# Half of a merge ahead of its last norms, a router that counts before it places, and a table product in the router's chain

## The chip, the cores and the metric

One Trainium2 chip, one core. The metric is the device time of one execution in microseconds, the median of several runs. The profiler takes one execution for the traces. TensorE (PE) does the matrix products, VectorE (DVE) and ScalarE (ACT) the elementwise work, GpSimd (POOL) index patterns and masks, SyncE (SP) issues most of the DMA transfers.

## The reference

256 tokens of width 1024 go through one block with a two-way recurrence, a neighbourhood attention and a mixture of 16 experts, and then through two further blocks. What bears on the change is this, in short:

```python
# first block
ya = rwkv_out(y, ...)               # per-head group norm of y (8 heads of 64), bonus, gate
x  = x + m2 * ((sigmoid(z9) * (ya @ proj_a) + sigmoid(z10) * (yb @ proj_b)) @ w_out)   # the merge
h2 = modulate(rms_norm(x), m3, m4)
x  = x + m5 * moe(h2, router_w, router_bias, w1, w3, w2)
# moe: scores = sigmoid(h2 @ router_w); the best of 4 expert groups, then its 2 best experts of 4;
# gate weights are the chosen scores, divided by their sum
for i in range(2):                  # the two further blocks
    h = h + mixer(rmsnorm(h))       # pooling and dilated attention
    h = h + square(relu(rmsnorm(h) @ w_up[i])) @ w_down[i]
    gate = sigmoid(rmsnorm(h) @ w_gate[i])
    h = h + gate * (p[i] @ w_ple[i])   # p: 256 tokens x 256, a table that depends on no earlier result
```

Everything is float32 on both sides.

## The kernel before

The stages follow each other on one core: the inputs' norm and the attention, the recurrence with the gate products and the second branch's projection beside it, the merge, the router and the experts, and then mixer, feed-forward and gate of the two further blocks.

**Precision.** A product of float32 accuracy is made as three fast products (`mm3`, L119 to L121) of operands that were split into a high part (ACT) and a rest (DVE). `split` (L127, L128) does this for small pieces; `prepare` (L180, L181) for the large weights, 128 x 2048 at a time, that `plan` lists and `advance` loads through SP's queue (L166). Some small products are plain float32 instead; the profile shows two records for each of those.

**Order.** A planner orders each engine's instructions by the order of emission and its own estimate of their times, so that text order is not engine order. `tc.issue_after(i)` forces a group of instructions behind `i` on the engine of `i`. Tiles with the same tag share a fixed number of buffers; a load into a tag waits until the oldest user is done.

**Recurrence and norms.** `rwkv` runs generators in turn: three slots of the recurrence, `gates` (gate products, L985 to L1024, a PSUM bank "gg"), `factors`, and `rwkv_out`. The latter makes four norms (`norm(t, g)`, L896 to L922: t is the token half, g the head group): PE transposes y, DVE and ACT normalise, PE transposes back (L918), and ACT and DVE split the result into `yaT` (L940, L941). The order is (1,0), (0,0), (1,1), (0,1), each as soon as its two units of the recurrence are past.

**Merge.** `merge` (L1139) multiplies `yaT` by `proj_a` in 4 column quarters q and 2 depth halves k2, `product(q, k2)` (L1146), 12 fast products each, 96 in all. The k2 = 0 products need only the norms with g = 0. Quarter by quarter, DVE and ACT then form `mT` (L1173 to L1176), `halves` multiplies it by `w_out`, and `done` adds the result to x. `feed` and `route` (L1737, L1749) transpose the new x and multiply it by the router's weights; `lg` are the router's logits.

**Router and experts.** `router` (L1205) is a chain of small DVE steps that ends with the mask of the chosen experts (`chose`) and the gate weights. `moe` (L1245) makes from it, with five plain products on PE, each token's place in its expert's list and the count by which an expert has more than 64 tokens (`more`). All engines then pass a branch on that count (L1293), behind which the overflow code lies. `experts` (L1406) prepares the gather: the rest of x's split (`rest`, L1428) and one-hot matrices from the places (`choose`, L1435), both ahead of the branch in the text, and then gathers the tokens of an expert group by products with the one-hots (L1461). `second_masks` makes masks for the mixer of the further blocks on POOL, in the text ahead of the gather. The transposes of x that start the experts' sums (L1268) stand ahead of the router in the text.

**Gate of a further block.** `second_gate` (L2001) loads p[i], transposes it (four transposes, L214), multiplies it by `w_ple_2[i]` in two column halves (24 products of 512 columns for both token halves), and uses these in `done` when the gate's own products end.

## Time and profile before

| what | value |
|---|---|
| median of 3 runs | 1576.36 us (1572.23, 1576.36, 1580.75) |
| the profiled execution | 1566.17 us |
| its span | 1564.5 us |
| mean granted TensorE clock | 0.966 of full speed |
| PE busy | 1457.9 us (93%), 10562 instructions |
| DVE busy | 889.1 us (57%), 1869 instructions |
| ACT busy | 634.8 us (41%), 1035 instructions |
| POOL busy | 306.6 us (20%), 316 instructions |
| moved by DMA | 274.21 MB |

The span is the time from the first to the last instruction of the profiled execution. In the rows of the trace, a line such as `L181 DVE TENSOR_TENSOR wl<-wr,wh 128x2048 fp32r<-128x2048 f32` names the line of the kernel, the engine, the operation, and output and inputs with partitions, elements and type. A bracket behind a row of the timeline tells how long the engine stood idle before and what released it. PEclk and the digits of the slices are shares of full speed and of the slice. DMA share is the mean busy share of the 16 DMA engines.

### The profile page before, as it was taken

How to read it: one execution, taken by the hardware profiler on the slowest of the kernel's cores; microseconds unless marked ns; L12 is line 12 of the kernel's file. 1: busy time of each engine (PE TensorE's matmuls, PEld its weight loads, DVE VectorE, ACT ScalarE, POOL GpSimd, SP SyncE). 2: the span in 40 equal slices, each digit the busy share in tenths (PEclk: the TensorE clock that was granted, in tenths of full speed). 3: DMA queues.
4: the chain of work that ended last, by engine and by line, in shares of the span. 5: the costliest groups of instructions: out<-in, count | busy, mean ns of one | idle time of the engine just before them, and what ended most of it. 6: DMA issues, size and time to landing. Idle time of an engine off the chain costs nothing.

```text
span 1564.5 us, 26010 instructions
## 1 busy us (share of the span) xinstructions
PE 1457.9 (93%) x10562; PEld 1113.8 (71%) x10562; DVE 889.1 (57%) x1869; ACT 634.8 (41%) x1035; POOL 306.6 (20%) x316
## 2 busy tenths in 40 slices
PE   6899999999999886689999899999999999999996
PEld 3677777778788675543443368699988887998885
DVE  3778458676766676622311255565556755755555
ACT  2433545444454452110110145554444645544443
POOL 1002049765666410490000000000000000000000
PEclk9899999898999897889999999999999999999999
DMA  9511223222232133689999935355554452555542
GB/s 325 162 42 66 68 84 122 79 80 73 69 94 77 56 134 129 258 331 420 421 419 421 380 98 173 108 170 185 186 187 168 155 197 87 183 189 188 188 162 74
DMA packets 118328, 274.21 MB, mean 175 GB/s; under 512 B 8591, under 2 KB 31795, under 8 KB 106935
## 3 DMA queue, kind: packets, MB, share of 16 engines
q1 hardware_dynamic: 115608, 270.13, 49.1%
q10 hardware_dynamic: 2559, 2.32, 0.5%
q8 instruction: 85, 1.39, 0.4%
q14 instruction: 44, 0.36, 0.1%
q0 software_dynamic: 32, 0.00, 0.0%
HBM read 271.36 MB, written 1.06 MB: 174 GB/s over the span
## 4 chain that ended last, share of the span: by engine, by line
PE 54%; DVE 1%; ACT 1%; issue 0%; DVEq 0%; ACTq 0%
PE mm L119 12%; PE mm L120 12%; PE mm L121 12%; PE mm L1476 11%; PE mm L1461 1%; PE mm L1619 1%; PE mm L1540 1%; PE mm L1876 1%; PE mm L1737 1%; PE mm L1895 1%; PE mm L1849 0%; PE mm L1905 0%; PE mm L214 0%; PE mm L1838 0%; DVE wl L181 0%
## 5 line engine op out<-in xcount | busy, mean ns | idle before, releaser
L181 DVE TENSOR_TENSOR wl<-wr,wh 128x2048 fp32r<-128x2048 f32 (+2 forms) x130 | 271.6, 2089 | 208.1 <-ACT wh L180 195.7
L180 ACT ACTIVATE wh<-wr 128x2048 fp32r<-128x2048 f32 (+2 forms) x130 | 227.2, 1749 | 160.7 <-PE mm L121 108.1
L121 PE MATMUL mm<-xTh,wl 128*128 128x256 f32 x512 | 143.9, 281 | 0.0
L120 PE MATMUL mm<-xTl,wh 128*128 128x256 f32 x512 | 143.7, 281 | 0.0
L119 PE MATMUL mm<-xTh,wh 128*128 128x256 f32 x512 | 143.2, 281 | 0.0
L119 PE MATMUL mm<-wh,fh 128*128 128x512 f32 x256 | 101.4, 396 | 0.0
L121 PE MATMUL mm<-wh,fl 128*128 128x512 f32 x256 | 101.1, 395 | 0.0
L120 PE MATMUL mm<-wl,fh 128*128 128x512 f32 x256 | 101.0, 395 | 0.0
L300 POOL TENSOR_SCALAR mr<-mr,silu_c 128x512 f32<-128x512 f32 x56 | 97.8, 1747 | 5.3 <-DMA mr<-in_mod_w_dram 5.1
L120 PEld LDWEIGHTS mm<-xTl,wh 128*128 128x128 f32 x512 | 96.2, 188 | 0.9 <-DVE xTl L941 0.3
L119 PEld LDWEIGHTS mm<-xTh,wh 128*128 128x128 f32 x512 | 96.1, 188 | 0.7
L119 PE MATMUL mm<-wh,xTh 128*128 128x512 f32 (+1 forms) x272 | 95.7, 352 | 0.7 <-ACT big L1813 0.5
L121 PEld LDWEIGHTS mm<-xTh,wl 128*128 128x128 f32 x512 | 96.3, 188 | 0.0
L120 PE MATMUL mm<-wl,xTh 128*128 128x512 f32 (+1 forms) x272 | 93.0, 342 | 0.0
L121 PE MATMUL mm<-wh,xTl 128*128 128x512 f32 (+1 forms) x272 | 92.5, 341 | 0.0
L301 POOL TENSOR_TENSOR mra<-mra,mr 128x512 f32<-128x512 f32 x56 | 74.0, 1322 | 4.2
L823 ACT ACTIVATE nt<-mm 128x512 f16<-128x512 f32 x80 | 47.6, 595 | 59.3 <-PE mm L837 51.8
L119 PEld LDWEIGHTS mm<-wh,xTh 128*128 128x128 f32 x272 | 51.2, 188 | 8.6 <-ACT big L1813 0.7
L121 PEld LDWEIGHTS mm<-wh,fl 128*128 128x128 f32 x256 | 48.1, 188 | 11.5
L120 PEld LDWEIGHTS mm<-wl,fh 128*128 128x128 f32 x256 | 48.1, 188 | 10.7
L119 PEld LDWEIGHTS mm<-wh,fh 128*128 128x128 f32 x256 | 48.1, 188 | 10.6
L121 PEld LDWEIGHTS mm<-wh,xTl 128*128 128x128 f32 x272 | 51.2, 188 | 6.2
(569 smaller groups left out, 3496.4 us busy)
## 6 DMA issues: line engine op xcount, KB each, us to landing
wr<-in_w_up_dram SPq DMA_DIRECT2D x32, 1024.0 KB, 5.6
wr<-in_w_down_dram SPq DMA_DIRECT2D x32, 1024.0 KB, 5.1
wr<-in_w_in_dram SPq DMA_DIRECT2D x22, 1024.0 KB, 5.1
wr<-in_moe_w_dram SPq DMA_DIRECT2D x21, 1024.0 KB, 8.7
wh<-in_moe_w_dram SPq DMA_DIRECT2D x20, 1024.0 KB, 13.8
wl<-in_moe_w_dram SPq DMA_DIRECT2D x20, 1024.0 KB, 12.0
mr<-in_mod_w_dram SPq DMA_DIRECT2D x64, 256.0 KB, 2.8
wx<-in_moe_w_dram SPq DMA_DIRECT2D x14, 1024.0 KB, 10.3
```

Source lines behind the costliest of these rows:

```text
L119: mm(out, l.hi, r.hi, start=start, stop=False, **kw)
L120: mm(out, l.hi, r.lo, start=False, stop=False, **kw)
L121: mm(out, l.lo, r.hi, start=False, stop=stop, **kw)
L180: self.nc.scalar.activation(w.hi, raw, AF.Copy)
L181: self.nc.vector.tensor_tensor(w.lo, raw, w.hi.bitcast(F32), op=ALU.subtract)
L300: nc.gpsimd.tensor_scalar(raw, raw, self.sc[:, k, 0:1], None, op0=ALU.mult)
L301: nc.gpsimd.tensor_tensor(acc, acc, raw, op=ALU.add)
L823: nc.scalar.activation(nt, v4(bz), AF.Copy)
L1461: mm(b[:, k * 256:k * 256 + 256], part[:, t, 2 * q + k, :], sel[:, t].rearrange("p j c -> p (j c)"), start=(i == 0), stop=(i == 3))
L1476: mm(b[r], lT[:, k0 + k, c0 + SLOT * j:c0 + SLOT * j + SLOT], w[:, k], start=(start and k == 0), stop=(stop and k == n - 1))
L1540: mm(acc[2 * n + k // 2][:, k % 2], part[:, k * P:(k + 1) * P], back, start=False, stop=(g == 7 and part is y.lo), skip_group_check=True)
L1619: mm(banks[t], first[:, k, t * P:(t + 1) * P], w[:, k, :], start=(k == 0), stop=False)
```

## The change

1. `merge` is taken apart into `merge_piece` (load and split a piece of `proj_a`) and `merge_product`. The four k2 = 0 products are issued in `rwkv_out`: two behind the first two norms, and one each with the third and the fourth. The norms now begin only when `gates` is past. The pieces have three split buffers instead of two.
2. The splits of the `w_out` weights (`prepare`) stand behind the last norm's own split.
3. The first further block's table product p[0] @ w_ple[0] moves ahead: p[0] is loaded at the start of the recurrence, w_ple[0] in the merge into tiles that the norms use until then, and eight plain float32 products run on PE behind the last `route`. ACT copies them out and stores them to DRAM; `second_gate(0)` loads them back in one transfer, and its transposes, products and weights are gone.
4. In `moe` the overflow count comes ahead of the places; x's transposes stand behind the place products; the gate weights are made behind the branch, and inside it for the overflow.
5. In `experts`, four of the eight `rest` steps are free, two stand behind the choice and two behind the one-hots; the one-hots of the first group are behind the branch, and `second_masks` behind the first gather.

The diff, cut to its core:

```diff
@@ rwkv_out
-            self.split_into(self.yaT[:, 2 * g:2 * g + 2, t * P:(t + 1) * P],
-                            b[:, 0:256].rearrange("p (k t) -> p k t", k=2))
+            dst, b = self.yaT[:, 2 * g:2 * g + 2, t * P:(t + 1) * P], b[:, 0:256].rearrange("p (k t) -> p k t", k=2)
+            self.normed = [nc.scalar.activation(dst.hi, b, AF.Copy).ins,
+                           tt(dst.lo, b, dst.hi.bitcast(F32), op=ALU.subtract).ins]
...
-        while not {("prep", d, g, i), "bonus"} <= self.past:
+        while not {("prep", d, g, i), "bonus", "gates"} <= self.past:
             yield
...
+        yield from until((0, 0, 3), (1, 0, 2))
+        yield from norm(1, 0)
+        yield from until((0, 0, 2), (1, 0, 3))
+        yield from norm(0, 0)
+        self.pieces = [self.merge_piece(fp, n) for n in range(3)]
+        for q, tag in enumerate(("gg", "nn1")):
+            self.merge_product(fp, q, 0, tag)
+            yield
+        yield from until((0, 1, 3), (1, 1, 2))
+        self.merge_product(fp, 2, 0, "nn2")
+        yield from norm(1, 1)
+        yield from until((0, 1, 2), (1, 1, 3))
+        self.merge_product(fp, 3, 0, "nn0")
+        yield from norm(0, 1)
@@ gates (three places: w of the gate products, of proj_b, and the end)
-                wt = self.split(pool, raw, [P, 2, 256], "w", bufs=2)
+                wt = self.split(pool, raw, [P, 2, 256], "w", bufs=3)
...
+        self.past.add("gates")
@@ merge
+    def merge_product(self, fp, q, k2, tag=None):
+        if tag:
+            self.merged.append(self.bank(tag, 1))
+        wt, b = self.pieces.pop(0), self.merged[q]
+        for k in range(2):
+            for j in range(2):
+                self.mm3(b[:, 256 * j:256 * j + 256], wt[:, k, j * P:(j + 1) * P], self.yaT[:, 2 * k2 + k, :],
+                         start=(k2 == k == j == 0), stop=(k2 == 1 and k == 1), skip_group_check=True)
+        n = 4 * k2 + q + 3
+        if n < 8:
+            self.pieces.append(self.merge_piece(fp, n))
...
+        for n in range(2):
             for k in range(2):
+                nc.sync.dma_start(ple[n][k], a["w_ple_2"][0][k * P:(k + 1) * P, 512 * n:512 * n + 512])
...
+        with self.tc.issue_after(self.normed[0]), self.tc.issue_after(self.normed[1]):
+            self.prepare()
...
+        self.ple = self.dram.tile([T, D], F32, name="pled")
+        for n in range(2):
+            banks = [self.bank(("nn1", "nn2")[t], 1) for t in range(2)]
+            with self.tc.issue_after(self.routed):
+                for t in range(2):
+                    for k in range(2):
+                        nc.tensor.matmul(banks[t], pT[:, k, t * P:(t + 1) * P], ple[n][k], start=(k == 0), stop=(k == 1))
+            for t in range(2):
+                o = fb.tile([P, 512], F32, tag=("mr", "mra")[n and t], name="pleo", bufs=(3, 1)[n and t])
+                nc.scalar.activation(o, banks[t], AF.Copy)
+                nc.scalar.dma_start(self.ple[t * P:(t + 1) * P, 512 * n:512 * n + 512], o)
@@ moe
+        score, mask = self.router(pool)
         left, more = pool.tile([1, 16], I32, name="left"), pool.tile([1, 1], I32, name="more")
         b = self.bank("mn")
         mm(b[:, 0:16], ones, mask[:, 0], start=True, stop=False)
         mm(b[:, 0:16], ones, mask[:, 1], start=False, stop=True)
         ts(left, b[0:1, 0:16], -float(SLOT), 0.0, op0=ALU.add, op1=ALU.max)
-        nc.vector.tensor_reduce(more, left, axis=AX.X, op=ALU.max)
+        found = nc.vector.tensor_reduce(more, left, axis=AX.X, op=ALU.max).ins
+
+        b = self.bank("mn")
+        mm(b[:, 0:16], tri, mask[:, 0], start=True, stop=True)
+        mm(b[:, 16:32], ones, mask[:, 0], start=True, stop=False)
+        placed = mm(b[:, 16:32], tri, mask[:, 1], start=False, stop=True).ins
+        place = pool.tile([P, 2, 16], F32, name="place")
+        with self.tc.issue_after(found):
+            stt(place, b[:, 0:32].rearrange("p (t e) -> p t e", t=2), 1.0, mask, op0=ALU.add, op1=ALU.mult)
+            ts(place, place, -1.0, None, op0=ALU.add)
+        with self.tc.issue_after(placed):
+            for k in range(8):
+                for t in range(2):
+                    mm(acc[k // 2][:, k % 2, t * P:(t + 1) * P], self.x[:, t, k * P:(k + 1) * P], self.ident,
+                       start=(k % 2 == t == 0), stop=False, skip_group_check=True)
...
-        run(self.second_masks(self.lys[1].tile([P, 8, T], F32R, tag="xTl", name="cmask", bufs=1).bitcast(F32)))
+        self.gate = self.weighed(pool0, score, mask)
         run(main)
@@ experts
+        rest(0, range(4))
         with self.tc.issue_after(self.chose):
-            rest(0)
+            rest(1, range(2))
+        yield
         with self.tc.issue_after(choose(0)):
-            for q in range(1, 4):
-                rest(q)
-        yield
+            rest(1, range(2, 4))
         for q in range(4):
             gather(0, q)
+
+        mask = self.lys[1].tile([P, 8, T], F32R, tag="xTl", name="cmask", bufs=1).bitcast(F32)
+        begin = nc.gpsimd.tensor_copy(mask[:, 7, 0:1], state["g", 0, 1][:, 3, 0:1]).ins
+        with self.tc.issue_after(begin):
+            run(self.second_masks(mask))
@@ second_gate
+        if i:
+            pt = ...
+        else:
+            done_ahead = pool.tile([P, 2, D], F32, name="ple")
+            nc.scalar.dma_start(done_ahead, self.ple[:, :].rearrange("(t p) d -> p t d", p=P))
...
+                if i == 0:
+                    state[t] = done_ahead[:, t, 512 * n:512 * n + 512]
+                    continue
```

## Rows read from the trace of the kernel before

**Rows 1.** The page's slices, 39.1 us each: TensorE's busy share in tenths.

```profile
PE   6899999999999886689999899999999999999996
```

**Rows 2.** Windows by stage; columns: window, length, busy by engine, PEclk, DMA share, GB/s.

```profile
576.00:606.00 30.00, 11.65 (x72) 10.11 (x73) 21.55 (x60) 8.63 (x11) 0.00 (x0) 0.63 0.76 265
...
604.00:617.00 13.00, 12.70 (x91) 12.57 (x92) 6.78 (x12) 4.69 (x8) 0.00 (x0) 0.85 0.20 62
...
617.00:644.00 27.00, 26.69 (x133) 21.73 (x132) 15.35 (x30) 5.99 (x10) 0.00 (x0) 1.00 0.45 161
...
650.00:657.00 7.00, 1.81 (x17) 1.61 (x15) 6.04 (x28) 2.28 (x2) 6.31 (x11) 0.91 1.01 411
...
720.00:730.00 10.00, 10.00 (x54) 4.52 (x54) 2.31 (x4) 1.83 (x3) 0.00 (x0) 1.00 1.01 418
...
1210.00:1214.00 4.00, 4.00 (x19) 3.25 (x18) 2.37 (x10) 2.08 (x2) 0.00 (x0) 1.00 0.63 194
```

**Rows 3.** Timeline of VectorE, tail and merge: start, us, instruction, idle before.

```profile
576.05 0.68 DVE L1024 SCALAR_TENSOR_TENSOR gt<-gt,mm 128x512 f32<-128x512 f32 x1
...
587.92 0.42 DVE L790 TENSOR_TENSOR y<-y,mm 128x256 f32<-128x256 f32 x1 [0.91 <-PE mm L784]
...
588.33 2.28 DVE L181 TENSOR_TENSOR wl<-wr,wh 128x2048 fp32r<-128x2048 f32 x1
...
605.41 0.42 DVE L941 TENSOR_TENSOR yaTa<-mm,yaTw 128x256 fp32r<-128x256 f32 x1 [1.26 <-ACT yaTw L940]
...
616.63 0.68 DVE L1176 TENSOR_TENSOR mTv<-mu,mTk 128x512 fp32r<-128x512 f32 x1
```

**Rows 4.** Timeline of TensorE, from the tail to the first gather.

```profile
556.60 1.02 PE L354 MATMUL mm<-con,thg 128*128 128x512 f32 x2
...
597.41 0.63 PE L898 MATMUL mm<-ident,y 128*128 128x128 f32 x2
...
604.61 0.56 PE L119 MATMUL mm<-yaTw,wh 128*128 128x256 f32 x1
...
647.99 3.82 PE L1268 MATMUL mm<-ident,xres 128*128 128x128 f32 x32
...
657.09 0.61 PE L1273 MATMUL mm<-o,row 128*128 128x16 f32 x2 [5.29 <-DVE o L1237]
...
669.76 0.77 PE L1461 MATMUL mm<-pick,xsh 128*128 128x256 f32 x2 [10.36 <-DVEq L1293]
```

**Rows 5.** Timeline of ScalarE in the tail.

```profile
581.70 1.91 ACT L180 ACTIVATE wh<-wr 128x2048 fp32r<-128x2048 f32 x1 [1.07 <-DMA wr<-in_w_out_dram]
```

**Rows 6.** Timeline of SyncE's queue, the first refill during the experts.

```profile
679.12 3.79 SPq L166 DMA_DIRECT2D wr<-in_moe_w_dram  x3
```

**Rows 7.** Timeline of ScalarE and VectorE, router, count and one-hots.

```profile
650.45 0.23 ACT L1211 ACTIVATE sc<-lg 128x32 f32<-128x32 f32 x1 [2.31 <-DVE lg L1193]
...
652.78 0.17 DVE L1228 TENSOR_TENSOR ing<-ing,g 128x8 f32<-128x8 f32 x1
...
659.68 0.15 DVE L1284 TENSOR_REDUCE more<-left 1x1 int32<-1x16 int32 x1
...
660.52 2.00 DVE L1435 TENSOR_SCALAR pick<-row,place 128x64 fp32r<-128x64 f32 x8
...
662.44 4.35 DVE L1428 SCALAR_TENSOR_TENSOR xsl<-xres,xr,xsh 128x256 fp32r<-128x256 f32 x6
...
666.71 2.00 DVE L1435 TENSOR_SCALAR pick<-row,place 128x64 fp32r<-128x64 f32 x8
```

**Rows 8.** The branch's line: duration (min/median/max, ns), first to last start, releaser.

```profile
L1293 PEldq COMPARE_BRANCH  x1: 3352/3352/3352, 660.5 to 660.5; - x1
...
L1293 DVEq EVENT_SEMAPHORE  x2: 21/21/21, 669.6 to 669.7; - x2
```

**Rows 9.** The chain of waits inside the first block's gate.

```profile
1214.67 0.24 PE mm L121
```

**Rows 10.** Groups of TensorE by line, 1202 to 1251 us: busy, mean ns.

```profile
L214 PE MATMUL mm<-ident,ple 128*128 128x128 f32 x4 | 0.6, 271 | 0.0
```

More of the change, by code (lines that the diff above doesn't have):

```diff
@@ L919, in norm, with until @@
                 nc.tensor.transpose(b[:, p * P:(p + 1) * P], y[:, p * P:(p + 1) * P], self.ident)
-            self.split_into(self.yaT[:, 2 * g:2 * g + 2, t * P:(t + 1) * P],
-                            b[:, 0:256].rearrange("p (k t) -> p k t", k=2))
+            dst, b = self.yaT[:, 2 * g:2 * g + 2, t * P:(t + 1) * P], b[:, 0:256].rearrange("p (k t) -> p k t", k=2)
+            self.normed = [nc.scalar.activation(dst.hi, b, AF.Copy).ins,
+                           tt(dst.lo, b, dst.hi.bitcast(F32), op=ALU.subtract).ins]
             yield
         i, d, g = units[-1]
-        while not {("prep", d, g, i), "bonus"} <= self.past:
+        while not {("prep", d, g, i), "bonus", "gates"} <= self.past:
             yield
+        self.merged = []
         self.yaT = Pair(*(self.zp.tile([P, 4, 256], F32R, tag=f"tl{n}", name=f"yaT{n}") for n in "wa"))
-        for g in range(2):
-            for t in (1, 0):
-                while not {(0, g, 2 + t), (1, g, 3 - t)} <= self.past:
-                    yield
-                yield from norm(t, g)
+        def until(*units):
+            while not set(units) <= self.past:
+                yield
[13 more added lines that the diff above has]
+        yield from norm(0, 1)
     def spare(self):
@@ L1265, in moe @@
         acc = [self.bank("ma", 4).rearrange("p (k t) -> p k t", k=2) for q in range(4)]
-        for k in range(8):
-            for t in range(2):
-                mm(acc[k // 2][:, k % 2, t * P:(t + 1) * P], self.x[:, t, k * P:(k + 1) * P], self.ident,
-                   start=(k % 2 == t == 0), stop=False, skip_group_check=True)
-        gate, mask = self.router(pool)
-        b = self.bank("mn")
-        mm(b[:, 0:16], tri, mask[:, 0], start=True, stop=True)
-        mm(b[:, 16:32], ones, mask[:, 0], start=True, stop=False)
-        mm(b[:, 16:32], tri, mask[:, 1], start=False, stop=True)
-        place = pool.tile([P, 2, 16], F32, name="place")
-        stt(place, b[:, 0:32].rearrange("p (t e) -> p t e", t=2), 1.0, mask, op0=ALU.add, op1=ALU.mult)
-        ts(place, place, -1.0, None, op0=ALU.add)
+        score, mask = self.router(pool)
         left, more = pool.tile([1, 16], I32, name="left"), pool.tile([1, 1], I32, name="more")
@@ L1283, in moe @@
         ts(left, b[0:1, 0:16], -float(SLOT), 0.0, op0=ALU.add, op1=ALU.max)
-        nc.vector.tensor_reduce(more, left, axis=AX.X, op=ALU.max)
+        found = nc.vector.tensor_reduce(more, left, axis=AX.X, op=ALU.max).ins
[9 more added lines that the diff above has]
+            for k in range(8):
+                for t in range(2):
+                    mm(acc[k // 2][:, k % 2, t * P:(t + 1) * P], self.x[:, t, k * P:(k + 1) * P], self.ident,
+                       start=(k % 2 == t == 0), stop=False, skip_group_check=True)
         self.rst.close()
         self.ly = self.lys[0]
-        args = acc, gate, place, row
-        main = self.experts(self.pool(st, "moe1"), st, *args)
+        main = self.experts(self.pool(st, "moe1"), st, acc, place, row)
         next(main)
@@ L1293, in moe @@
             with self.tc.If(some(more) > 0):
+                args = acc, self.weighed(pool, score, mask), place, row
                 for e in range(16):
@@ L1401, in layer_pieces, with experts @@
             for n in range(2):
-                out += self.blocks(a["w_ple_2"][i], 512 * n, 512, 2)
+                if i:
+                    out += self.blocks(a["w_ple_2"][i], 512 * n, 512, 2)
                 out += self.blocks(a["w_gate_2"][i], 512 * n, 512)
         return out
-    def experts(self, pool1, st, acc, gate, place, row):
+    def experts(self, pool1, st, acc, place, row):
         nc, a = self.nc, self.a
@@ L1421, in experts, with rest @@
                 nc.scalar.activation(hi, raw, AF.Copy, scale=self.rs[t])
-        def rest(q):
-            for t in range(2):
+        def rest(t, qs):
+            for q in qs:
                 raw, hi, lo = (ap[:, 2 * q:2 * q + 2] for ap in (self.x[:, t].rearrange("p (q k) -> p k q", k=8),
```

90 lines of the change are left out of this document (49 added, 41 removed).

## The prediction

> **What bounds the kernel now.** I read the slices first: behind the start, TensorE is busy nine tenths or more almost throughout, but falls to 8, 8, 6, 6 and 8 tenths in five slices from 508 to 704 us, 39.1 us each [rows 1]. The windows part these into two dips with a full stretch between, and show the later stages [rows 2]. In 576 to 606 PE works 11.65 of 30 us while DVE is busy 21.55: that is the end of the recurrence, its two last output norms. From 617 to 644 (output projection) PE is full. From 650 to 657 it works 1.81 of 7 us, with DVE at 6.04 and POOL at 6.31: the experts are chosen; and the first gather at 669.76 ends a wait of 10.36 us [rows 4]. Behind that the experts run with PE at 10.00 of 10 us and the DMA engines at 1.01, and the second gate with PE at 4.00 of 4. So two kinds of gain exist: time in the two dips, where the latest chain of DVE, ACT and PE decides, and PE work taken out of a full stretch. I then followed the chain in each dip by its timeline.
>
> **The tail and the merge.** The last recurrence output y is ready at 588.34 (587.92 + 0.42), the last norm's transpose starts at 597.41 and its split yaT lands at 605.83 (605.41 + 0.42) [rows 3, 4]: one norm takes 8.4 us. In the same stretch DVE runs three weight splits of 2.28 us, 6.84 together, among the norms' small steps [rows 3]. PE starts the merge products at 604.61 [rows 4] and from there has no gap: 12.70 of 13 us in 604 to 617, then 26.69 of 27 [rows 2]. The 96 merge products come first, then the output projection.
>
> The change does three things here. (1) The w_out splits go behind the last norm. If all three stand in the chain, yaT comes at 605.83 - 6.84 = 599.0; the chain alone allows 588.34 + 8.4 = 596.7; and it could stay at 605.83 if other work fills the places. (2) Half of the products (48 of 96) run between the norms, where PE is mostly idle. By 12.70 us for 91 records [rows 2] they are 48 x 0.14 = 6.7 us; all of it is hidden there if yaT's first half is early. (3) The splits must now be paid behind the norm: the first group of w_out needs an ACT split of 1.91 [rows 5] and a DVE split of 2.28 [rows 3]. DVE also owes the mT quarters, three operations of 0.68 each [rows 3], of which two quarters (4.1 us) come before the projection can run on. With 0.8 for the hops between engines that makes 1.91 + 2.28 + 4.1 + 0.8 = 9.1 us from yaT to the projection; the remaining 48 products (6 us) lie inside it.
>
> Before: 96 x 0.14 = 13.4 us from 604.61; records of the projection's first products are interleaved at the end, so I take 13.0, and the projection starts, in effect, at 617.6. After: 599.0 + 9.1 = 608.1. That is 9.5 us. I take 8: the first norms now wait for the gates, whose last DVE step starts at 576.05 [rows 3], and so two norms move into 576 to 606, each of 22 DVE steps at about 0.25 (between the 0.17 of a small step [rows 7] and the 0.42 of one of 256 columns [rows 3]), 5.4 us, with three proj_a splits of 0.7 (512 columns, as in the mT row). DVE has 30 - 21.55 + 6.84 = 15.3 us free there, 12.9 are used, and some of this will be in a norm's way. Bounds: yaT not earlier than before, 617.6 - 605.8 - 9.1 = 2.7; yaT at 596.7, 11.8. On SP's queue four loads of the table weights (256 KB each) wait for tiles that only the last norm frees. Behind them stand one proj_a piece, used 5 us or more after yaT, and the later weight loads; those of the experts find full buffers until 679 anyway [rows 6]. I cost this at nothing; if the piece is late its 12 products slip by a load, about 2 us.
>
> **The router's chain.** It runs from ACT's score at 650.45 to the first place product at 657.09 [rows 4, 7], then the counts to 659.83 (659.68 + 0.15) [rows 7], the branch, and the first gather at 669.76 [rows 4].
> - Masks. POOL is busy 6.31 of 7 us in 650 to 657 [rows 2], building masks that nobody needs until the second mixer. The chain's 24 or so small steps cost 0.17 to 0.2 each by the short ones [rows 7], 4.9 us, against the 6.6 seen. The mask work goes behind the first gather. I take 1.0 from [0 to 1.5]. The Trainium skill ("SBUF — State Buffer", Who interferes with whom) says that DVE's second port is shared with GpSimd and that the loser blocks for the whole instruction; by that rule all of the 1.7 us could return, and the same rule speaks against the new place, where POOL's masks would stand beside the experts' DVE work. No row separates this, and PE sets that stage.
> - Count first. Five fp32 products and their DVE reads lie between 657.09 and 659.68 [rows 4, 7]; two products are enough for the count: 3 x 0.43 = 1.3.
> - Branch. From the count to the gather it takes 669.76 - 659.83 = 9.93 us. DVE gets there late: it first runs one-hots (2.00), six rests of the split (4.35) and another 2.00 of one-hots [rows 7], and the events behind its branch come at 669.6 [rows 8], 0.1 before the gather. The other engines pay a branch of 3.35 us (PE) [rows 8]. Afterwards DVE has the place and little else, so: 0.65 to the branch, 3.35 through it, 0.2, and the one-hots 2.00, which now stand behind it: 6.2 to 6.3. Gain 3.6. If the planner hoists one-hots and rests ahead of the branch again, 1.2; if the one-hots overlap the fetch, 5.5.
> - Against that, four rests are freed and two stand right behind the choice; one of 0.7 between choice and count costs 0.7.
> - Table products: 8 plain fp32 products of 512 columns. The row for one has 1.02 us (two records) [rows 4], so at most 8.2 from about 647, which ends when the choice does (656); PE had the x transposes there (3.82 us from 647.99 [rows 4]), and those go under the branch, where PE is idle for 10 us. At half the clock the products would run some 6 us into the counts. I cost them at nothing, and keep that in the low end. Four ACT copies and stores are hidden beside them: ACT is busy 2.28 of 7 us.
> - The gate weights move behind the branch, on DVE, ahead of a product that comes ten microseconds later: nothing.
>
> Sum: 1.0 + 1.3 + 3.6 - 0.7 = 5.2, bounds 1 and 8.
>
> **The experts.** PE and the DMA engines are both full there [rows 2]. The stream restarts when the first up products free their buffers, at 679.12 [rows 6], and these follow the gather; so the stage starts earlier as a whole and keeps its length.
>
> **The second gate, first block.** 24 products of 512 columns leave (2 halves x 2 token tiles x 2 of k x 3), 0.24 each on the chain [rows 9], 24 x 0.235 = 5.6, and four transposes, 0.6 [rows 10]. PE has no gap there [rows 2], so all of it counts: 6.2, bounds 5 and 6.5. In their place comes one load of 1 MB: 2.5 us at the 418 GB/s of a full stretch, more beside the 194 GB/s of weights that this one carries [rows 2], and it is needed only behind the first 36 gate products (8.4 us).
>
> **Sum.** 8 + 5.2 + 6.2 = 19.4. The profiled execution took 1566.17 us; it would take 1546.8. It is 10.2 below the median shown, 1576.36, and my forecast goes by that median: 1557.
>
> **The rivals.**
> - A. The tail stays full of DVE work: norms behind the gates, splits of yaT and of proj_a fill the freed slots, yaT comes no earlier. For it: DVE is the busiest engine there. Against: 15 us of free room for 13. Gain 2.5 + 5.2 + 6.2 = 13.9, time 1562.5.
> - B. What the front gains is given back in the experts, because the transfers, not the gather, set their end: DMA is at 1.01 of its time and 418 GB/s [rows 2]. Against: the queue itself waits for the first up products. If B holds, only the gate's 6.2 stay: 1570.
> - C, the other side. The norms wait for the gates and then run one after another with a piece of proj_a, a piece of waiting and 8.4 to 12.1 us each: 576.7 + 4 x 12.1 + 8 x 0.69 = 630.6 for yaT instead of 605.8, and the time is about 1587. It loses only when yaT is later than 605.8 + 2.7 + 5.2 + 6.2 = 619.9. For it: the wait is for the whole gates, not for a norm's own unit. Against: the gates end at 576.7, 12 us before the last y, and the norms' steps can interleave.
> - D. The planner puts one-hots or rests ahead of the branch again, as it did for the second group (666.71) [rows 7]: the router gives 1 of its 5.2, time 1561.
>
> **How the numbers follow.** The forecast of 1557 has 0.58 (its own range 1549 to 1564, the sums of half the bounds), A 0.15, D 0.09, B 0.08, C 0.05, and a gain of over 25 us, with the upper bounds in all three places, 0.05. The range takes in the forecast, A, D and, by half, B, and leaves out C and most of the larger gain: 1546 to 1572. A measurement of this kernel tells about 0.5%, 7.9 us, from no change. Faster by more than that are the forecast, A, D and the larger gain, less the slow edge of A: 0.82; B and that edge are within it: 0.13; slower is C, 0.05.
>
> **What would show it.** After the change: no weight split of 2048 columns on DVE before the last yaT, and yaT at 597 to 602; half of the merge products before it; the projection from about 608, without a gap. In the router: POOL idle until the first gather, no transposes of x ahead of the count, gather 6 to 7 us behind the count; the table products ending before the choice. In the gate: no table products, and PE still without a gap while the reload lands. Wrong would be: yaT after 606, a gap on PE behind yaT of more than 10 us, DVE operations between count and branch, or the expert stage longer by what the front won.

## The result and the profile after

The changed kernel is slower: 1582.52 us median of 20 runs (1571.81 to 1588.81) against 1571.58 of 20 runs of the kernel before (1559.33 to 1580.75). The ratio is 1.0075, 95% interval 1.0056 to 1.0095. The profiled execution took 1571.81 us, its span is 1570.1, its mean clock 0.969; so the trace is that of the fastest run, 10.7 us below the median. Six runs of later experiments fell into a slower state and are left out of every median and ratio below.

The tail, timeline of VectorE (start, us, instruction, idle before):

```profile
575.63 0.69 DVE L1039 SCALAR_TENSOR_TENSOR gt<-gt,mm 128x512 f32<-128x512 f32 x1 [0.46 <-PE mm L121]
...
578.90 0.42 DVE L790 TENSOR_TENSOR y<-y,mm 128x256 f32<-128x256 f32 x1 [1.08 <-PE mm L784]
579.24 0.42 DVE L903 TENSOR_REDUCE mu<-mm 128x4 f32<-128x256 f32 x1
...
586.30 0.42 DVE L922 TENSOR_TENSOR yaTa<-mm,yaTw 128x256 fp32r<-128x256 f32 x1 [1.26 <-ACT yaTw L921]
...
610.39 0.42 DVE L922 TENSOR_TENSOR yaTa<-mm,yaTw 128x256 fp32r<-128x256 f32 x1 [1.26 <-ACT yaTw L921]
612.18 2.29 DVE L181 TENSOR_TENSOR wl<-wr,wh 128x2048 fp32r<-128x2048 f32 x1 [1.37 <-ACT wh L180]
```

The last y is ready at 579.32, 9.0 us earlier than in [rows 3]. But no norm has begun: the first starts at 579.24, and the four stand in a row, the first from 579.24 to 586.72, 7.4 to 7.5 us where nothing comes between. The last yaT lands at 610.81, 5.0 later than in [rows 3]. In the kernel before, two norms were over long before the last y (588.34), beside the recurrence; their ends on VectorE:

```profile
570.70 0.41 DVE L941 TENSOR_TENSOR yaTa<-mm,yaTw 128x256 fp32r<-128x256 f32 x1
...
580.66 0.42 DVE L941 TENSOR_TENSOR yaTa<-mm,yaTw 128x256 fp32r<-128x256 f32 x1 [0.95 <-ACT yaTw L940]
```

TensorE in the changed kernel, the timeline from there on:

```profile
609.73 3.44 PE L1247 MATMUL mm<-rw,fac 128*128 128x16 f32 x16
613.00 0.78 PE L119 MATMUL mm<-yaTw,wh 128*128 128x256 f32 x2
...
621.35 0.48 PE L119 MATMUL mm<-wh,mTk 128*128 128x512 f32 x1
...
654.41 7.21 PE L1236 MATMUL mm<-ple,pT 128*128 128x512 f32 x16
661.99 0.39 PE L1322 MATMUL mm<-o,ones 128*128 128x16 f32 x2 [0.37 <-DVE o L1284]
...
680.62 0.76 PE L1516 MATMUL mm<-pick,xsh 128*128 128x256 f32 x2 [13.67 <-DVEq L1347]
```

Half of the merge products did run between the norms. But the router's input products (16 records) now stand behind the last norm, and the projection starts at 621.35 where 608.1 was forecast. In the trace of before these products stood here:

```profile
576.79 1.96 PE L1200 MATMUL mm<-rw,fac 128*128 128x16 f32 x16 [0.92 <-DVE gt L1024]
```

TensorE's granted clock is also at its lower level for longer. These are windows behind the last norm, first in the kernel before, then in the changed one (columns as in [rows 2]):

```profile
604.61:607.90 3.29, 3.29 (x17) 3.29 (x16) 0.42 (x1) 0.90 (x2) 0.00 (x0) 0.50 0.03 5
...
609.73:617.80 8.07, 8.07 (x39) 8.07 (x39) 4.36 (x5) 5.97 (x6) 0.00 (x0) 0.50 0.45 141
```

The 8.07 us at half of full speed would be about 4 at full speed (an estimate from the clock alone); before, there were 3.29 such us. Later the projection also waits 1.8 us for pieces of mT that stand behind the w_out splits on VectorE, a wait that the trace of before does not have. The table products take 7.21 us and end with the choice, as forecast. The gather is at 680.62, 10.9 later than in [rows 4].

Why the gather is late shows on ScalarE:

```profile
656.73 0.23 ACT L1258 ACTIVATE sc<-lg 128x32 f32<-128x32 f32 x1 [4.21 <-DVE lg L1228]
657.27 0.60 ACT L1239 ACTIVATE pleo<-mm 128x512 f32<-128x512 f32 x1 [0.31 <-PE mm L1236]
657.90 0.35 ACTq L1240 DMA_DIRECT2D pled<-pleo  x1
...
666.49 0.60 ACT L1239 ACTIVATE pleo<-mm 128x512 f32<-128x512 f32 x1 [7.52 <-DMA pled<-pleo]
...
667.99 2.12 ACT L1476 ACTIVATE xsh<-xres,xr 128x1024 fp32r<-128x1024 f32 x1
670.00 2.13 ACT L1476 ACTIVATE xsh<-xres,xr 128x1024 fp32r<-128x1024 f32 x1
```

and on VectorE:

```profile
661.52 0.19 DVE L1275 TENSOR_TENSOR o<-o,g 128x32 f32<-128x32 f32 x1
...
662.92 0.16 DVE L1325 TENSOR_REDUCE more<-left 1x1 int32<-1x16 int32 x1
...
670.14 2.42 DVE L1483 SCALAR_TENSOR_TENSOR xsl<-xres,xr,xsh 128x256 fp32r<-128x256 f32 x4 [6.41 <-ACT xsh L1476]
...
676.09 0.90 DVE L1490 TENSOR_SCALAR pick<-row,place 128x64 fp32r<-128x64 f32 x5
680.67 0.58 DVE L1490 TENSOR_SCALAR pick<-row,place 128x64 fp32r<-128x64 f32 x3 [3.69 <-DVEq L1347]
```

The third table copy waits 7.52 us for the first copy's store (the one store whose landing this trace shows by itself landed 8.4 us after its issue). The high parts of x stand behind it in ACT's queue and come 11.3 us behind the score; before, one stood ahead of the score (650.45) and one right behind it:

```profile
646.01 2.14 ACT L1421 ACTIVATE xsh<-xres,xr 128x1024 fp32r<-128x1024 f32 x1
...
650.59 2.14 ACT L1421 ACTIVATE xsh<-xres,xr 128x1024 fp32r<-128x1024 f32 x1
```

The rests need them, the branch stands behind the rests on VectorE, and PE's gather is released by VectorE's event behind the branch. All eight one-hots of the first group and five of the second still stand ahead of the branch.

### The profile page after: what moved, and what is told of

It is laid out like the page before. It is cut to its first block, busy times and chain, and to the rows that moved or that the text cites. A ratio compares the mean times of both kernels' runs of the same rounds, so it can differ in the third digit from the quotient of the medians.

```text
span 1570.1 us, 26009 instructions
## 1 busy us (share of the span) xinstructions
PE 1456.6 (93%) x10554; PEld 1109.0 (71%) x10554; DVE 883.7 (56%) x1865; ACT 633.6 (40%) x1037; POOL 306.1 (19%) x317
## 4 chain that ended last, share of the span: by engine, by line
PE 54%; DVE 1%; ACT 1%; issue 0%; DVEq 0%; ACTq 0%
PE mm L119 12%; PE mm L120 12%; PE mm L121 12%; PE mm L1531 11%; PE mm L1516 1%; PE mm L1679 1%; PE mm L1595 1%; PE mm L1937 1%; PE mm L1797 1%; PE mm L1956 1%; PE mm L1910 0%; PE mm L1966 0%; PE mm L214 0%; PE mm L1899 0%; PE mm L1918 0%
## 5 line engine op out<-in xcount | busy, mean ns | idle before, releaser
L120 PEld LDWEIGHTS mm<-wl,fh 128*128 128x128 f32 x256 | 48.2, 188 | 10.8
L119 PEld LDWEIGHTS mm<-wh,fh 128*128 128x128 f32 x256 | 48.1, 188 | 10.6
## 6 DMA issues: line engine op xcount, KB each, us to landing
wh<-in_moe_w_dram SPq DMA_DIRECT2D x20, 1024.0 KB, 11.8
```

Of the source, the lines that this page charges most:

```text
L119: mm(out, l.hi, r.hi, start=start, stop=False, **kw)
L120: mm(out, l.hi, r.lo, start=False, stop=False, **kw)
```

## How the runs are compared

The stretch up to the end of the recurrence varies from run to run with the granted clock (by 20 us between the profiles below), also between kernels that have the same instructions there. So times of a profile are counted from one event ahead of the change: the end of the last addition but one to y (L790; 568.82 in the kernel before, 568.10 in the changed one). "To the end" is the span less that event. In the kernel before, most of the first norm lies ahead of this event, so that what its move frees there is in no column. A column comes from one profiled execution, and it is not free of the clock: behind the event the granted clock was 0.974 in the trace of before and 0.971 in that of the changed kernel. The clock is the median over the runs of the kernel; runs of one kernel whose mean clock differs by 0.001 differ by 1.3 us.

| kernel | ratio to before (95%) | clock | last yaT | score | count | gather | first up | to the end |
|---|---|---|---|---|---|---|---|---|
| before | | 0.963 | 37.0 | 81.6 | 91.0 | 100.9 | 105.3 | 995.7 |
| changed | 1.0075 (1.0056 to 1.0095) | 0.9595 | 42.7 | 88.6 | 95.0 | 112.5 | 116.2 | 1002.0 |
| e1_norms_free | 1.0051 (1.0021 to 1.0081) | 0.961 | 38.6 | 84.5 | 90.9 | 108.2 | 111.9 | 997.8 |
| e2_store_free | 1.0031 (0.9994 to 1.0069) | 0.9615 | 42.7 | 88.5 | 106.0 | 114.5 | 118.0 | 996.7 |
| e3_no_table | 1.0056 (1.003 to 1.0081) | 0.962 | 42.4 | 90.1 | 97.3 | 105.1 | 107.2 | 998.7 |
| e5_old_merge | 0.9988 (0.9964 to 1.0013) | 0.9655 | 36.9 | 81.9 | 89.2 | 105.2 | 108.9 | 995.3 |
| e6_old_router | 1.015 (1.0109 to 1.019) | 0.9595 | 43.2 | 90.4 | 106.8 | 115.2 | 120.1 | 1014.8 |
| e7_two_buffers | 1.0043 (1.0013 to 1.0073) | 0.963 | 42.8 | 90.0 | 97.3 | 113.0 | 116.7 | 1003.2 |
| e8_before_three_buffers | 1.0052 (1.0017 to 1.0087) | 0.959 | 37.9 | 82.5 | 91.9 | 103.1 | 108.5 | 999.5 |
| e12_three_again | 1.0069 (1.0038 to 1.01) | 0.960 | 38.0 | 84.3 | 93.4 | 104.7 | 110.1 | 1001.1 |
| e16_before_space | 1.0004 (0.9983 to 1.0025) | 0.9625 | 37.0 | 81.8 | 91.1 | 102.5 | 107.7 | 998.4 |
| e9_old_merge_free_store | 0.9954 (0.992 to 0.9987) | 0.962 | 37.9 | 82.8 | 94.5 | 102.8 | 106.5 | 986.1 |
| e10_before_pad | 0.9986 (0.9962 to 1.0011) | 0.959 | 36.9 | 81.6 | 91.0 | 100.1 | 104.9 | 989.8 |
| e11_router_alone | 0.9972 (0.9949 to 0.9995) | 0.965 | 36.9 | 83.5 | 90.7 | 99.0 | 101.0 | 992.0 |
| e13_half_table | 0.9951 (0.9927 to 0.9976) | 0.966 | 36.9 | 81.6 | 99.6 | 108.3 | 110.4 | 992.7 |
| e14_half_elsewhere | 0.9952 (0.992 to 0.9984) | 0.9635 | 36.9 | 81.8 | 92.5 | 101.3 | 103.3 | 985.8 |
| e15_router_pad | 0.992 (0.9889 to 0.9951) | 0.967 | 37.9 | 84.2 | 91.4 | 99.9 | 102.0 | 989.1 |

For the changed kernel the columns differ from those of before by +7.0 at the score, +4.6 more at the gather (23.9 against 19.3 behind the score), -0.7 at the first up product, +2.4 from there to the first mixer's scores (963.62 before, 976.16 after), and -6.9 from there to the end. That is +6.3 in the columns. The runs' mean clock, 0.9598 against 0.9636, is worth 0.0038 x 1.3 per 0.001 = 5.0 us. Together that is 11.3, and the medians differ by 10.9; as the columns hold some clock too, the sum is a rough one. The runs alone say the same: the mean times, 1581.7 against 1570.9 (111 runs of the kernel before, beside the experiments), are 10.8 apart, and less the clock's 5.0 that leaves 5.8.

## The experiments

Theory: the tail costs time because the norms stand in a row behind the gates, and the router because ACT waits for a store. Rivals: VectorE has the same work in any order; the one-hots ahead of the branch cost the time, not the copies.

**The norms' wait moved behind the second norm (e1_norms_free).**

```diff
-        while not {("prep", d, g, i), "bonus", "gates"} <= self.past:
+        while not {("prep", d, g, i), "bonus"} <= self.past:
...
         yield from norm(0, 0)
+        yield from until("gates")
         self.pieces = [self.merge_piece(fp, n) for n in range(3)]
```

> The changed kernel, but the first two norms no longer wait for the gates; the wait stands behind the second norm, ahead of the merge pieces. Theory (the tail is long because all four norms of 7.4 us stand in a row behind the gates): the two early norms go back beside the recurrence, the last yaT comes 4 to 10 us earlier than 610.8, the score 4 to 8 earlier than 656.7, and the time falls by 4 to 8 from that of the changed kernel, to 1.002 to 1.005 of the kernel before. Rival (DVE has the same work in the tail in either order, so the recurrence's last y gets later by what the norms get earlier): yaT within 2 us of 610.8, time as the changed kernel, 1.0075.

Counted from the event, yaT came 4.1 earlier, the score 4.1 and the gather 4.3; 1.0051. In the schedule the theory holds. The time fell by 0.24%, 3.8 us, just short of the 4 to 8, and its interval takes in 1.0075, so the time alone does not separate the two. The score is still 2.9 later than before, with yaT only 1.6 later: the projection stands behind the router's input products, part of them and of the merge products at half clock, and waits 1.8 us for the mT pieces behind the w_out splits, as in the changed kernel. No run separates these.

**The table product back in the gate (e3_no_table).**

```diff
-        self.ple = self.dram.tile([T, D], F32, name="pled")
-        for n in range(2):
-            banks = ...
```

(with its loads, its transposes and the reload; `second_gate` as before.)

> The changed kernel without the early table product: second_gate computes p[0] @ w_ple[0] in its place as in the kernel before; everything else as changed. Theory (ACT's table copies wait 7.5 us for a store to DRAM and hold up x's high parts, these the rests, and these the branch and the gather): the high parts stand beside the score again, and the gather comes some 10 us behind the count, 6 to 9 earlier than 680.6; the gate gets its 6.3 back, so the time falls by 0 to 3 from that of the changed kernel, to 1.0055 to 1.0075. Rival (the one-hots and rests ahead of the branch cost the time, not the copies): the gather stays 15 us or more behind the count, and the time rises by 4 to 6, to 1.010 to 1.0115.

ScalarE in this run, timeline:

```profile
658.39 2.13 ACT L1453 ACTIVATE xsh<-xres,xr 128x1024 fp32r<-128x1024 f32 x1
664.50 0.23 ACT L1236 ACTIVATE sc<-lg 128x32 f32<-128x32 f32 x1 [3.99 <-DVE lg L1218]
664.64 2.11 ACT L1453 ACTIVATE xsh<-xres,xr 128x1024 fp32r<-128x1024 f32 x1
```

The high parts stand around the score again, and the gather is 15.0 behind it instead of 23.9. So the early table costs the router 8.9 us from the score to the gather. Counted from the event it is 7.4, for the score itself is 1.5 later here (why is told under e11). It gives the gate 6.1 (321.5 us between the two mixers' first scores here, 315.4 with it). The rival falls, for all 16 one-hots of the first two groups stand ahead of the branch in this run.

**The old merge (e5_old_merge), and the old router (e6_old_router).** The one puts `gates`, `rwkv_out` and the merge products back, the other `router`, `moe` and `experts`; the rest is as changed. In short:

```diff
-        with self.tc.issue_after(self.normed[0]), self.tc.issue_after(self.normed[1]):
-            self.prepare()
-            self.merge_product(fp, q, 1)
+            product(q, 1)
```

```diff
-        self.gate = self.weighed(pool0, score, mask)
+        run(self.second_masks(self.lys[1].tile([P, 8, T], F32R, tag="xTl", name="cmask", bufs=1).bitcast(F32)))
         run(main)
```

> The changed kernel with the merge of before: norms, merge products, pieces with two buffers, w_out splits and router inputs in their old places; table product and router as changed. Theory (the new order of norms and merge costs 6 us by the score): the score comes back to 650 to 652, the time falls by 4 to 7 from that of the changed kernel, to 1.003 to 1.005. Rival (the merge is neutral and all of the loss lies behind the score): time as the changed kernel, 1.0075.

The score came back to 81.9, and the time to that of the kernel before, further than expected: with the old merge the two split buffers are back as well, and the clock is 0.9655. The merge part, its third buffer included, is the larger part of the loss.

> The changed kernel with router, count, branch and experts in the order of before (masks on POOL beside the choice, five products ahead of the branch); merge and early table product as changed. Theory (the store that ACT waits for sets the gather in both orders): choice 1.5 to 2 us longer, count 1.3 to 1.7 later, the gather at 680 or later, time up by 0 to 4, to 1.0075 to 1.010. Rival (the new order of the router costs the time between count and gather): gather 4 us or more earlier than 680.6, time down by 4 to 6, to 1.0035 to 1.005.

Slower by another 0.75%, outside both expectations. The gather did not come earlier and the count came 11.8 later, so the new order is not what costs. The run also has a loss of its own, which undoing this part alone brings in: the experts' weight stream stood still. The waits of SyncE's queue in this run:

```profile
SPq L166 <- POOL band L1757: 29.4, 1, 29.4
```

The masks that POOL makes ahead of the experts in this order held a tile that a weight load wanted.

**Table copies that reuse no tile (e2_store_free).**

```diff
-                o = fb.tile([P, 512], F32, tag=("mr", "mra")[n and t], name="pleo", bufs=(3, 1)[n and t])
+                if n == 0:
+                    o = self.gp.tile([P, 512], F32, tag=f"y{t}", name="pleo")
+                else:
+                    o = fb.tile([P, 512], F32, tag=("mr", "mra")[t], name="pleo", bufs=(3, 1)[t])
```

(and the score issued ahead of the copies.)

> The changed kernel, but the first two table copies on ACT go to two tiles that the merge has done with, so that the third copy reuses no tile whose store is still under way; the score is issued ahead of the copies. Theory (the 7.5 us wait of ACT for that store holds up the high parts, the rests and the gather): no wait of ACT for a store, the high parts 4 to 5 us earlier against the score (11.3 behind it in the changed kernel), the gather 4 to 6 earlier (23.9 behind the score), time down by 4 to 6 from that of the changed kernel, to 1.004 to 1.005. Rival (the one-hots and rests ahead of the branch decide): the gather moves by 2 us at most, time within 2 us of the changed kernel, 1.0065 to 1.0075.

This expectation fell: ACT waits no more, the high parts come 5.3 us behind the score, but the gather came 26.0 behind it, later than before the repair. The wait had moved. VectorE in this run:

```profile
673.96 0.67 DVE L1489 SCALAR_TENSOR_TENSOR xsl<-xres,xr,xsh 128x256 fp32r<-128x256 f32 x1 [8.44 <-DMA pled<-pleo]
...
680.28 0.15 DVE L1331 TENSOR_REDUCE more<-left 1x1 int32<-1x16 int32 x1
```

The first rest writes a tile of the experts, and that takes the memory of a copy whose store is still under way; the count stands behind it. That the whole time fell all the same comes from the added 128 bytes (below).

**Two buffers (e7), three buffers alone (e8, e12), and only their space (e16).** In the first four runs, those with the new merge lost more than their columns account for. The edit of e7, which also loads two pieces ahead instead of three; e8 and e12 (the same kernel twice) are its reverse in the kernel before:

```diff
-                wt = self.split(pool, raw, [P, 2, 256], "w", bufs=3)
+                wt = self.split(pool, raw, [P, 2, 256], "w", bufs=2)
```

> The changed kernel with two split buffers for the pieces instead of three, in the gates and in the merge, and two pieces ahead instead of three. What the tail, the router and the gate of the kernels measured so far account for leaves some 7 us that every kernel with the new gates and merge has and the one with the old merge does not. Theory (the third buffer lengthens the recurrence by 5 us or so): time down by 4 to 6 from that of the changed kernel, to 1.0035 to 1.005. Rival (the buffers do nothing there): within 2 us of the changed kernel, 1.0065 to 1.0085.

> The kernel before with three split buffers instead of two for the pieces of the gates and the merge, and nothing else. Theory of the third buffer: 4 to 6 us slower than the kernel before, 1.0025 to 1.004. Rival: no difference, 0.9985 to 1.0015.

> The kernel before with three split buffers in the gates and the merge, once more, on whatever chip this is: its first run gave 1.0052 (1.0017 to 1.0087), and its profile shows the same length of the recurrence's last parts at full clock as the kernel before. Theory (the third buffer costs 4 to 8 us): 1.0025 to 1.006. Rival (the granted clock of the runs differed by chance): 0.998 to 1.002.

The last of these, in `gates`:

```diff
+        pad = pool.tile([P, 1024], F32, name="pad")
+        nc.gpsimd.memset(pad[:, 0:1], 0.0)
         for q in range(8):
```

> The kernel before with an unused tile of 4 KB a partition (the size of the third split buffer) in the pool of the gates' pieces, two buffers as before. Theory (the space shifts later tiles and that costs the time): 1.004 to 1.007, median clock 0.957 to 0.960. Rival (the splits that run further ahead cost it): 0.998 to 1.002, median clock 0.962 to 0.965.

Three buffers alone made the kernel before slower twice, by 0.52 and 0.69%, at a median clock of 0.959 and 0.960; two buffers in the changed kernel brought the clock back to 0.963 and the time to 1.0043, while its columns stayed (1003.2 to the end). The columns of e8 and e12 to the end, 999.5 and 1001.1, are longer as well, though the instructions are the same; the granted clock behind the event was 0.969 and 0.964 in these traces, against 0.974. The same space without the buffer did nothing (1.0004). What remains, by exclusion, is that the splits may run further ahead, and what is seen of it is a lower clock. Why that lowers it stays open: between the sixth and the eighth gate piece, the pieces are 35.1 and 36.2 us apart in every profile, with two buffers or three.

**The old merge with the free store (e9), 128 bytes (e10), and the router alone (e11).** The first is the edits of e5 and e2 together, the third those of e5 and e3; the second is this:

```diff
         nc.gpsimd.memset(self.ones, 1.0)
+        self.pad = c.tile([P, 2, 16], F32, name="pad")
+        nc.gpsimd.memset(self.pad, 0.0)
```

> Both repairs: the merge of before (as in the run with the old merge, 0.9988) and the table copies that wait for no store; early table product and new order of the router stay. Theory: the gather comes 4 to 6 us earlier against the score than in the run with the old merge (23.4 behind it), time 0.994 to 0.996. Rival (the one-hots ahead of the branch decide): 0.998 to 0.999.

> The kernel before with one more small tile (128 bytes a partition, set to zero on POOL at the start and read by nobody) in the pool that lives through the whole program, so that later tiles stand 128 bytes higher. In the two runs with the copies that wait for no store, which hold such a tile, the feed-forward stages took 157.3 us instead of 159.0 and the part from the first mixer's scores to the end 588 to 590 instead of 594, with the same instructions. Theory (where the tiles stand sets the pace of the large products): that part falls from 600.9 to 595 to 596, time 0.996 to 0.9975. Rival (something else in those two kernels did it): that part within 1 us of 600.9, time 0.9985 to 1.0015.

From the first mixer's scores to the end e10 took 595.3 instead of 600.9. Its ratio, 0.9986, settles no gain by itself: its clock was 0.959. A group of the run's products (1080 to 1180 us; busy, mean ns):

```profile
L119 PE MATMUL mm<-wh,fh 128*128 128x512 f32 x78 | 30.4, 390 | 0.0
```

The same window of the kernel before, at the same full clock:

```profile
L119 PE MATMUL mm<-wh,fh 128*128 128x512 f32 x66 | 26.0, 394 | 0.0
```

All six traces with such a tile (e2, e9, e10, e13, e14, e15) have 390 there; the kernel before, the changed one, e8, e11, e12 and e16 have 394 to 395. The 0.9954 of e9 is this and the gate: its gather is 20.0 behind the score, so its router gained nothing, and the time lies in the theory's range without the theory's cause.

> The kernel before with the new order of router, count, branch and experts alone: old merge, table product in the gate. Theory (the prediction's router term of 5.2 us is right where no table copy stands in ACT's queue): high parts beside the score, the first gather 14 to 16 us behind the score instead of 19.3, the first up product 4 to 7 us earlier against the score, time 0.996 to 0.998. Rival (the one-hots that the planner still puts ahead of the branch eat the gain): gather 18 to 20 behind the score, time 0.9985 to 1.0015.

In e11 the gather is 15.5 behind the score instead of 19.3, and the first up product 17.5 instead of 23.7; 0.9972. The router's term exists where no copy stands in ACT's queue. But the score itself is 1.9 later. The four rests that the change frees need the first high part alone, and with ACT's queue clear they run ahead of the logits (`lg`) of the second token half. VectorE in e11:

```profile
651.53 0.66 DVE L1435 SCALAR_TENSOR_TENSOR xsl<-xres,xr,xsh 128x256 fp32r<-128x256 f32 x1
...
654.12 0.23 DVE L1193 SCALAR_TENSOR_TENSOR lg<-mm,xr,rsh 128x16 f32<-128x16 f32 x1
```

So from the event the gather gains 1.9 and the first up product 4.3. In e3 and e15 the rests stand there too; in the changed kernel they do not, for their high part is late.

**Half of the table (e13), and where its copies stand (e14).** Both start from e9. Only the first column half is made early; in e14 its two copies stand in memory that the experts do not take.

```diff
-        for n in range(2):
+        for n in range(1):
...
-        with self.tc.issue_after(self.chose):
+        with self.tc.issue_after(self.found):
             rest(1, range(2))
```

```diff
-                    o = self.gp.tile([P, 512], F32, tag=f"y{t}", name="pleo")
+                o = self.rt.tile([P, 512], F32, name=f"pleo{t}")
```

> A version made from the findings: old merge, new order of the router with the two rests behind the count instead of behind the choice, the score ahead of the table copies, and only the first column half of the table product early (two copies on ACT that wait for no store), the other half in the gate; the score's tile also shifts later tiles by 128 bytes. Theory: gather 14 to 17 us behind the score, half of the gate's 6.3, and the shift's 5: time 0.990 to 0.994. Rival (two copies ahead of the high parts still cost what the gate gives): 0.995 to 0.998.

> The run with half of the table product early, but its two copies on ACT go to tiles in memory that the experts' tiles do not take over. Theory (VectorE's first rest waited 9.4 us for the store of a copy to land, because x's split parts take that memory): no such wait, the count 6 to 9 us earlier against the score than the 18.0 of that run, the gather 17 to 20 behind the score instead of 26.7, time 0.989 to 0.992. Rival (the high parts behind the two copies are late anyway): gather 23 or more behind the score, time 0.994 to 0.996.

The theory of e13 fell: the gather is 26.7 behind the score, not 14 to 17, and the time 0.9951. The first rest in e13 and in e14:

```profile
658.37 0.67 DVE L1464 SCALAR_TENSOR_TENSOR xsl<-xres,xr,xsh 128x256 fp32r<-128x256 f32 x1 [9.39 <-DMA pled<-pleo]
```

```profile
664.50 0.67 DVE L1461 SCALAR_TENSOR_TENSOR xsl<-xres,xr,xsh 128x256 fp32r<-128x256 f32 x1 [2.07 <-ACT xsh L1454]
```

The wait for the store is gone, the count comes 10.7 behind the score instead of 18.0, the gather 19.5 instead of 26.7, and 6.9 us are saved to the end. That shows the landing of the stores as the cause of the wait. The medians don't show it (0.9951 and 0.9952, short of the 0.989 to 0.992 expected of e14): the clock was 0.966 in the one and 0.9635 in the other, worth 3 us, and the rest is within their intervals. The rival is right in part: the high parts behind the copies still hold the choice for 2.07 us.

**The version that the findings point to (e15_router_pad):** the kernel before with the new router and 128 bytes more, the edits of e11 and e10.

> The new order of the router alone (as in the run with 0.9972) plus the unused tile of 128 bytes at the start (0.9986 alone). Theory (both add up): first up product 4 us earlier against the recurrence's last parts, first mixer's scores to the end 595 to 596 instead of 600.9, time 0.992 to 0.9955. Rival (the faster pace lowers the granted clock, as that run's median clock of 0.959 against 0.963 may say, and gives it back): 0.996 to 0.998.

0.992, 13 us faster than the kernel before and 24 faster than the changed one. Not all of the 13 is the edit's: to the end it is 6.6 us, nearly all from the first mixer's scores on (595.0 instead of 600.9). Of the 3.4 gained at the first up product 0.7 is left at those scores. Some 5 us go with the runs' clock, 0.967 against 0.963. The rival fell, for the clock is not lower; but why it was higher than in the runs of e10, which has the same bytes, is not shown, and with six runs this part may be luck.

## Why the prediction was wrong

Forecast were 19.4 us less; measured were 10.9 more, outside the range. Point by point:

- **Tail and merge: forecast -8, measured +7.0 at the score.** The step that failed is the one that put the two early norms into VectorE's free time between 576 and 606, at 5.4 us of work each (half of the second lay there already). That VectorE would have room was right: from 576.00 to 610.81 it was busy 24.15 of 34.81 us. But a norm is a chain of single steps that takes 7.4 us by itself, and behind the gates the four stood one behind the other. In the kernel before, the first had ended at 571.11 and the second at 581.08, beside the recurrence; the recurrence ended 9.0 earlier without them, and that was worth less than the row of four cost. The run with the two norms moved back (e1) brought 4.1 us back. This is rival C, held at 0.05. Its mechanism was right and its price five times too high (yaT at 630.6 against 610.8), because it took 12.1 us for a norm, a length measured while other work was mixed in. That C's time lies 10.6 us above the median it went by, and the measured one 10.9, is luck: the router and the clock made up what C had too much. From yaT to the score the chain is 1.3 longer than before, though 48 products fewer remain there. What the prediction did not list is that the router's input products give up their own bank and stand behind the last norm (3.44 us), that TensorE runs these and part of the remaining products at half clock, and that mT waits behind the w_out splits on VectorE. So the 9.1 us from yaT to the projection came out at 10.5.
- **Router: forecast -5.2, measured +4.6 from the score to the gather.** Count first and the masks did what was said: score to count 6.4 instead of 9.4. The step that failed costed ACT's copies and stores at nothing because ACT was busy 2.28 of 7 us. Busy time was not the question; the queue was: what stands behind the third copy, and what that copy waits for. Without the table the term is real, 3.8 us to the gather, but half of it goes to the free rests ahead of the score (1.9 us net, e11); the prediction costed only a rest between choice and count. Rival D's mechanism was right as well: the one-hots stayed ahead of the branch in every order, and the count-to-gather stretch shrank by 1.6 (9.9 to 8.3, the router alone), near the 1.2 given for it.
- **The masks: forecast 1.0.** From the score to the end of the choice it is 5.2 us instead of 6.6. One step of the choice, 128x32 elements, took 0.76 us beside POOL in the kernel before and 0.19 with POOL idle (661.52 above):

```profile
656.04 0.72 POOL L1692 TENSOR_TENSOR cmask<-cmask 128x256 f32<-128x256 f32 x1
...
656.05 0.76 DVE L1228 TENSOR_TENSOR o<-o,g 128x32 f32<-128x32 f32 x1
```

The step ended just behind POOL's. The Trainium skill ("SBUF — State Buffer", Who interferes with whom) says that a VectorE instruction with two inputs in SBUF contends with a GpSimd instruction that reads SBUF, over one port pair that is locked exclusively. These two rows agree with it; not every such step is held up, the next one, at 656.85, took 0.19. In the masks' new place nothing was lost that a row shows: in e11, which has them there, the stretch from the first up product to the first mixer's scores is 290.4 us instead of 289.5.
- **Experts: forecast unchanged.** They kept their length but for 2.4 us. Rival B could not show here, for the front gained nothing that could be given back. Where it gained, the runs differ: of 4.3 us at the first up product e11 kept 3.4 at the first mixer's scores, of 3.4 e15 kept 0.7. So B is open.
- **Gate: forecast -6.2.** From the first to the second mixer's scores it is 315.4 instead of 321.6: -6.2. The reload landed in 4.9 us, hidden, as said.
- **The clock and the third buffer** were in no term of the sum. The lower clock is worth 5.0 us, about as much as the schedule lost. It goes with the third buffer: two buffers brought it back (e7), three alone lowered it (e8, e12). How a buffer does that is open.

## What to carry to other kernels

An engine with little work is not a free place for work: look at what its queue will hold behind the new instruction, and at what the new instruction waits for, a store's landing and the memory that the next tiles take over included. Work taken out of an overlapped stretch shortens the stretch and lengthens what follows: cost a chain that is to run later at its length alone, times the number that now stand in a row, and not by the work that it is for the engine. Compare profiles from an event ahead of the change, and list the mean clock of the runs beside the ratio; a tuning step can show no longer schedule and still be slower.

## What the runs showed of the hardware

128 bytes more ahead of all later tiles made the 512-column products 390 ns instead of 394 at full clock, and the feed-forward stage of the first further block, from the first down product to the gate's first, 157.8 us instead of 159.4, with the same instructions. Three split buffers instead of two, with the same instructions on every engine, ran at a mean clock of 0.957 to 0.9585 instead of 0.9636. A 256 KB store from SBUF to DRAM landed 8.4 us after its issue in the changed kernel and between 5.8 and 8.9 in the other runs, and its tile's memory was busy for that time: VectorE waited 8.44 us (e2) and 9.39 us (e13) to write there.
